# Two fp32r products of a split operand in place of one fp32 product for the row sums of an RWKV-7 recurrence

## The chip, the cores and the metric

One core of a Trainium2 chip. The metric is the device time of one execution in microseconds. Engines are named as the profile names them: PE is TensorE (PEld its weight loads), DVE is VectorE, ACT is ScalarE, POOL is GpSimd, SP is SyncE, which here only issues DMAs.

## What is computed

Two transformer blocks on one sequence of 1024 tokens of width 1024. The first has differential attention beside a diagonal state-space layer and a gated feed-forward; the second has multi-scale retention beside an RWKV-7 recurrence, a gated feed-forward and a gated embedding. All is fp32. The change lies in the RWKV-7 recurrence, which has 8 heads of 64 columns. Two sums over the 64 columns of a head stand in it: the norm of the key, and the bonus.

```python
    kk = k * k_k.reshape(H, N)
    kk = kk * lax.rsqrt(jnp.maximum(jnp.sum(kk * kk, axis=-1, keepdims=True), 1e-24))
    ...
    bonus = jnp.sum(r * k * r_k, axis=-1, keepdims=True) * v
```

## The kernel before

The kernel runs phase after phase. Large matmuls are done as three fp32r products (high by high, high by low, low by high) of operands that were split into a high and a low fp32r part: `split` (L103, L104) writes the high part on ScalarE with an ACTIVATE copy and the low part on VectorE as a subtraction, and `mm3` (L149) issues the three products. Small matmuls of the recurrence are single fp32 products.

`phase_mixers` is the stage of the change. The recurrence is computed in chunks of 64 tokens, on 2 heads at a time: 16 rounds of 4 chunks (4 pairs of heads, 4 quarters of the sequence). Each round goes through four generators: `rw_pre` prepares the round's operands, `rw_solve` inverts a triangular system by substitution and doubling, `rw_chain` carries the state from chunk to chunk, `rw_tail` normalizes and stores. In step i the stage interleaves `rw_pre` of round i, `rw_solve` of round i - 1, `rw_chain` of i - 2 and `rw_tail` of i - 3, and, as filler on TensorE, the retention heads (`ret_all`) and the projections of the next pair of heads (`rw_proj`), whose matmuls are those of L149. `merge` takes turns among the generators by weights (PRN = 40 for `rw_pre`), one `yield` at a time; `ahead` raises the priority of the recurrence's generators. The order on each engine then follows from a scheduler that is run when the kernel is built and that knows dependences, buffers and priorities, so it depends on the whole program.

The rows of a head lie on partitions in `rw_pre`: a tile is 128 partitions (2 heads of 64 columns) by 256 tokens. A sum over a head's columns is therefore a matmul with `C["bones"]`, a 128x128 matrix of ones in two diagonal blocks of 64, and comes out on all 64 partitions. There are two such products in each round. The first (L1475) sums u, the square of the scaled key, written by ScalarE (L1473); its result goes to `d` (L1478), to the reciprocals (L1481), and on to `AR`, `KB`, `AA` and, through a DMA to memory and back, to `A`, on which `rw_solve` of the round begins. The second (L1537) sums u = r * rkw * u (L1535, VectorE), where u before was k times a factor (L1503); its result goes to `bv` (L1540), which only `rw_tail` needs. The tile u has two buffers (UBF = 2). Both results lie in PSUM tiles with the tag `r0`, which has two buffers for `rw_pre`, `rw_solve` and `rw_tail` together. The pool `rw` holds the recurrence's tiles; the pool `rkv`, with the tiles of the projections, lies behind it.

Of the kernel before, what the change touches and what calls it, by code (L numbers as in the profile page):

```python
# [11 lines left out]
F32R = mybir.dt.float32r  # L12
# [54 lines left out]
class Builder:  # L67
# [1351 lines left out]
    def rw_proj(self, pr, hT, pk, pt, ps):  # L1419
# [3 lines left out]
        for i, n in enumerate("rkv"):  # L1423
            ws[n] = self.wunit(self.I["w_rw"][2 + 3 * pr + i])
            for hf in range(2):
# [7 lines left out]
                out[n, hf] = x  # L1433
                yield

    def rw_pre(self, n, p, ps, B, D):


# [2 lines left out]
        nc = self.nc  # L1441
        V, G, AC, TE = nc.vector, nc.gpsimd, nc.scalar, nc.tensor
# [11 lines left out]
        def tmp(tag, bufs=1):  # L1454
            return self.t(p, [128, 256], tag=tag, bufs=bufs)
# [15 lines left out]
        yield  # L1471
        u = tmp("u", UBF)
        AC.activation(u, k, AF.Square, scale=kkw)  # L1473
        pd = self.t(ps, [128, 256], tag="r0", bufs=2)
        TE.matmul(pd, self.C["bones"], u, start=True, stop=True)  # L1475
        yield
        d = tmp("d")
        V.tensor_scalar(d, pd, 1e-24, None, ALU.max)  # L1478
# [21 lines left out]
        u = tmp("u", UBF)  # L1500
# [32 lines left out]
        AC.copy(KBt.rearrange("p c h k -> p c (h k)"), pt)  # L1533
        yield
        V.scalar_tensor_tensor(u, r, rkw, u, ALU.mult, ALU.mult)  # L1535
        pb = self.t(ps, [128, 256], tag="r0", bufs=2)
        TE.matmul(pb, self.C["bones"], u, start=True, stop=True)  # L1537
        yield
        bv = D["bv"] = tmp("bv", BVB)
        V.tensor_tensor(bv, v, pb, ALU.mult)  # L1540
# [325 lines left out]

    def phase_mixers(self, hT):

        with ExitStack() as s:
            p = self.pool("rw", 1, None, s)  # L1870
            pk = self.pool("rkv", 4, None, s)
            ps = self.pool("rwps", 1, PSUM, s)
            B = {}
            B["reset"] = self.load_const("reset", p)
            B["mask"] = self.load_const("rwmask", p).rearrange("p (m t) -> p m t", m=2)
            B["blk"] = self.load_const("rwblk", p).rearrange("p (m b) -> p m b", m=2)
            B["tinit"] = self.load_const("tinit", p).rearrange("p (a b) -> p a b", a=4)
            self.rkv = {}
            D = [{} for _ in range(16)]

            def step(i, *more):
                gens = []
                if 0 <= i - 2 < 16:
                    gens.append((self.ahead(self.rw_chain(i - 2, p, ps, B, D[i - 2]), HC), CHN))
                if 0 <= i - 3 < 16 and i != 16:
                    gens.append((self.ahead(self.rw_tail(i - 3, p, ps, D[i - 3]), HT), TLN))
                if 0 <= i - 1 < 16:
                    gens.append((self.ahead(self.rw_solve(i - 1, p, ps, B, D[i - 1]), HS), SON))
                if i < 16:
                    gens.append((self.ahead(self.rw_pre(i, p, ps, B, D[i]), HP), PRN))  # L1890
                self.merge(gens + [(self.some(g, n), n * FIL) for g, n in more])

            with ExitStack() as s2:
                pw = self.pool("wraw", 1, None, s2, "right") if FINE else None
                self.ws = self.wpool("wD", 2, FINE or 1, s2, "right", pw)
                wr = self.wpool("wR", WRB, FINE or 1, s2, "right", pw)
                pr = self.pool("ret", 1, None, s2, "right")
                self.C2 = {n: self.load_const(n, pr) for n in ("rsc",)}
                ret = self.ahead(self.ret_all(hT, wr, pr, ps), HR) if HR else self.ret_all(hT, wr, pr, ps)
                self.merge([(self.rw_proj(0, hT, pk, pr, ps), 1)])  # L1900
                for i in range(16):
                    if i % 4 == 0 and i < 12:
                        proj = self.rw_proj(i // 4 + 1, hT, pk, pr, ps)
                    step(i, (ret, RS[i]), *([(proj, PJ)] if i < 12 else []))
                self.merge([(ret, 1)])
                self.merge([(self.ahead(self.rw_tail(13, p, ps, D[13]), HT), 1)])
            ct = [self.h_half() for _ in range(2)]
            hT = self.new_hT()
            self.acc = []
            with ExitStack() as s2:  # L1910
                self.acc_half("right")
                self.pn = self.pool("norm", 1, None, self.end, "right")
                self.t(self.pn, [128, 96], tag="pad")
                pe = self.pool("wE", 8, None, s2, "right")
                pws = (pk, "rkv", RKV), (pe, "w"), (pe, "w")
                tags = (("mm", 2), ("mm", 2), ("rt", 2), ("rt", 2))
                early = itertools.chain(
                    self.o_load(0, ct[0], range(8), pk, "rkv", RKV),
                    self.o_half(0, ct[0], pws, (("rkv", RKV),), pk, ps, tags, self.acc, OG),
                    self.o_load(1, ct[1], range(7), pk, "rkv", RKV))  # L1920
                for i in (16, 17, 18):
                    step(i, (early, OE))
                self.merge([(early, 1)])
        return ct[1], hT
# [303 lines left out]
```

## Time and profile before

| | |
|---|---|
| median of 3 runs | 2813.11 us (2798.59 to 2817.27) |
| the profiled execution | 2815.24 us, of which the span is 2813.5 us |
| busy share of the span | PE 96%, PEld 80%, DVE 63%, ACT 40%, POOL 22% |
| mean granted TensorE clock | 0.979 of 2.4 GHz |

The profile is of one execution. Busy times are those of instruction records; a matmul's record is longer than the time for which it holds the array, since matmuls are pipelined, so how far matmuls are apart is read from the starts. Rows of the timeline merge equal instructions that follow one another: the length of such a row reaches from the first one's start to the last one's end.

### The profile page before, as it was taken

How to read it: one execution, taken by the hardware profiler on the slowest of the kernel's cores; microseconds unless marked ns; L12 is line 12 of the kernel's file. 1: busy time of each engine (PE TensorE's matmuls, PEld its weight loads, DVE VectorE, ACT ScalarE, POOL GpSimd, SP SyncE). 2: the span in 40 equal slices, each digit the busy share in tenths (PEclk: the TensorE clock that was granted, in tenths of full speed). 3: DMA queues.
4: the chain of work that ended last, by engine and by line, in shares of the span. 5: the costliest groups of instructions: out<-in, count | busy, mean ns of one | idle time of the engine just before them, and what ended most of it. 6: DMA issues, size and time to landing. Idle time of an engine off the chain costs nothing.

```text
span 2813.5 us, 44349 instructions
## 1 busy us (share of the span) xinstructions
PE 2707.0 (96%) x16624; PEld 2258.4 (80%) x16624; DVE 1763.0 (63%) x3481; ACT 1136.1 (40%) x2210; POOL 627.9 (22%) x1096
## 2 busy tenths in 40 slices
PE   7999998999999999999999999998899999999998
PEld 6988887877888888887787788886787878888887
DVE  6655668377757765464567676766557576665463
ACT  4233566444323344445333333333434233344352
POOL 5024533144111110021132241434031111110010
PEclk9999998999999999999999999999999999999999
DMA  4111020242455566555211111214614555586532
GB/s 144 43 46 48 21 76 23 92 150 90 164 184 175 168 219 236 190 187 188 87 52 43 53 55 47 68 41 135 223 53 135 187 171 170 172 283 204 171 126 85
DMA packets 173807, 352.10 MB, mean 125 GB/s; under 512 B 37784, under 2 KB 83064, under 8 KB 173592
## 3 DMA queue, kind: packets, MB, share of 16 engines
q1 hardware_dynamic: 152248, 277.43, 30.1%
q0 software_dynamic: 21344, 71.84, 7.2%
q8 instruction: 130, 2.13, 0.3%
q14 instruction: 85, 0.70, 0.1%
HBM read 246.90 MB, written 102.30 MB: 124 GB/s over the span
## 4 chain that ended last, share of the span: by engine, by line
PE 68%; issue 11%; DVE 8%; DMA 6%; POOL 3%; ACT 3%; SPq 0%; POOLq 0%; DVEq 0%; ACTq 0%
PE y L149 19%; PE mm L149 15%; PE x L149 7%; PE o L149 6%; PE z L149 5%; PE tr L149 3%; DVE w L104 1%; PE r L1514 1%; PE tr L200 1%; DMA raw<-w_ffn 1%; POOL rp L641 1%; DMA As<-ds 1%; PE o L758 1%; PE u L149 1%; PE r L1604 1%
## 5 line engine op out<-in xcount | busy, mean ns | idle before, releaser
L103 ACT ACTIVATE w<-raw 128x1024 fp32r<-128x1024 f32 (+1 forms) x324 | 286.4, 890 | 418.1 <-PE y L149 147.5
L104 DVE TENSOR_TENSOR w<-raw,w 128x1024 fp32r<-128x1024 f32 (+1 forms) x324 | 331.6, 1028 | 136.3 <-ACT w L103 129.1
L149 PE MATMUL y<-h,w 128*128 128x512 f32 x1152 | 288.6, 392 | 5.4 <-DVE v L353 4.1
L149 PE MATMUL y<-w,h 128*128 128x512 f32 x1152 | 267.3, 391 | 0.0
L149 PE MATMUL mm<-w,h 128*128 128x256 f32 (+1 forms) x1632 | 258.7, 300 | 8.2 <-ACT w L103 7.8
L149 PEld LDWEIGHTS y<-h,w 128*128 128x128 f32 x1152 | 216.5, 189 | 53.1 <-DVE v L353 6.0
L149 PEld LDWEIGHTS y<-w,h 128*128 128x128 f32 x1152 | 215.1, 188 | 44.4 <-ACT mix L1260 0.3
L149 PEld LDWEIGHTS mm<-w,h 128*128 128x128 f32 x1632 | 220.7, 191 | 28.1 <-ACT w L103 8.2
L149 PE MATMUL y<-hx,w 128*128 128x512 f32 x960 | 233.6, 391 | 1.1 <-ACT hx L103 0.9
L149 PEld LDWEIGHTS y<-hx,w 128*128 128x128 f32 x960 | 180.6, 189 | 40.4 <-ACT hx L103 1.8
L149 PE MATMUL mm<-h,w 128*128 128x512 f32 x672 | 188.3, 416 | 6.1 <-ACT w L103 3.0
L104 DVE TENSOR_TENSOR h<-dr,h 128x512 fp32r<-128x512 f32 x154 | 102.3, 687 | 137.5 <-ACT h L103 132.6
L149 PE MATMUL o<-w,h 128*128 128x512 f32 x768 | 182.0, 394 | 2.7 <-DVE mix L1270 1.5
L149 PE MATMUL x<-h,w 128*128 128x512 f32 x672 | 175.3, 392 | 0.0
L149 PEld LDWEIGHTS o<-w,h 128*128 128x128 f32 x768 | 142.5, 188 | 33.1 <-DVE mix L1270 2.2
L103 ACT ACTIVATE h<-dr 128x512 fp32r<-128x512 f32 x154 | 92.6, 624 | 176.3 <-DMA dr<-ff 77.3
L149 PE MATMUL mm<-w,xh 128*128 128x256 f32 x768 | 158.0, 301 | 4.6 <-ACT qk L631 3.4
L149 PEld LDWEIGHTS mm<-h,w 128*128 128x128 f32 x672 | 122.1, 194 | 35.0 <-ACT w L103 4.1
L149 PEld LDWEIGHTS x<-h,w 128*128 128x128 f32 x672 | 124.9, 188 | 26.1 <-ACT w L103 0.9
L149 PE MATMUL z<-h,w 128*128 128x512 f32 x576 | 143.2, 396 | 2.4 <-ACT s L367 1.6
L251 POOL DMA_DIRECT2D ff<-v x66 | 36.4, 551 | 481.6 <-DVE v L361 474.0
L376 DVE TENSOR_TENSOR t<-raw,raw 128x512 f32<-128x512 f32 x40 | 29.8, 744 | 178.0 <-DMA raw<-w_ffn 178.0
(527 smaller groups left out, 5464.8 us busy)
## 6 DMA issues: line engine op xcount, KB each, us to landing
raw<-w_ffn SPq DMA_DIRECT2D x88, 512.0 KB
dr<-ff SPq DMA_DIRECT2D x70, 512.0 KB
ff<-v POOLq DMA_DIRECT2D x88, 256.0 KB, 3.1
td<-w_dn SPq DMA_DIRECT2D x44, 512.0 KB
td<-td POOLq DMA_DIRECT2D x44, 512.0 KB, 3.7
raw<-td SPq DMA_DIRECT2D x40, 512.0 KB
ff<-sd POOLq DMA_DIRECT2D x66, 256.0 KB, 4.8
raw<-w_dn SPq DMA_DIRECT2D x30, 512.0 KB
```

Of the source, the lines that this page charges most:

```text
L103: self.nc.scalar.activation(hi, src, AF.Copy)
L104: self.nc.vector.tensor_tensor(lo, src, hi, ALU.subtract)
L149: return self.nc.tensor.matmul(*a, **kw, skip_group_check=more)
L200: nc.tensor.transpose(p[:, 128 * j : 128 * j + 128], xs[j][:, 128 * k : 128 * k + 128], self.ident)
L251: self.store("v").dma_start(self.part(("ff", {(0, 0): 0, (1, 0): 1, (1, 1): 2}[m, n]), f // 2), v)
L376: V.tensor_tensor(t[:, lo], r[1][:, lo], r[0][:, lo], ALU.subtract)
L641: nc.gpsimd.tensor_tensor(o, a, b, ALU.mult)
L758: nc.tensor.matmul(po, l, r, start=l is am, stop=False)
L1514: TE.matmul(pa[:, c].rearrange("p m t -> p (m t)"), KB[q, c].rearrange("p m s -> p (m s)"), AR[q, c].rearrange("p m t -> p (m t)"), start= ...
L1604: px = per(lambda o, h, c: TE.matmul(o, E[H[h], c], W[H[h], c], start=True, stop=True))
```

## The change

The two fp32 products go through a new helper, `head_sums`. It splits the operand u into an fp32r high part and an fp32r low part (`split`, one instruction on ScalarE and one on VectorE, each 128x256) and issues two fp32r products with the ones, which add up in one PSUM tile. The tiles uh and ul are in the pool `rw`, one buffer each, 1 KB per partition each. The ones are copied to fp32r once at the stage's start (VectorE, 128x128, 512 bytes per partition). Ahead of each of the two PSUM tiles one `yield` is added.

```diff
--- before.py
+++ after.py
@@ -1433,6 +1433,13 @@
                 out[n, hf] = x
                 yield
 
+    def head_sums(self, out, u, p, B):
+
+        uh, ul = (self.t(p, [128, 256], F32R, n) for n in ("uh", "ul"))
+        self.split(uh, ul, u)
+        self.nc.tensor.matmul(out, B["bones"], uh, start=True, stop=False)
+        self.nc.tensor.matmul(out, B["bones"], ul, start=False, stop=True)
+
     def rw_pre(self, n, p, ps, B, D):
 
 
@@ -1471,8 +1478,9 @@
         yield
         u = tmp("u", UBF)
         AC.activation(u, k, AF.Square, scale=kkw)
+        yield
         pd = self.t(ps, [128, 256], tag="r0", bufs=2)
-        TE.matmul(pd, self.C["bones"], u, start=True, stop=True)
+        self.head_sums(pd, u, p, B)
         yield
         d = tmp("d")
         V.tensor_scalar(d, pd, 1e-24, None, ALU.max)
@@ -1533,8 +1541,9 @@
         AC.copy(KBt.rearrange("p c h k -> p c (h k)"), pt)
         yield
         V.scalar_tensor_tensor(u, r, rkw, u, ALU.mult, ALU.mult)
+        yield
         pb = self.t(ps, [128, 256], tag="r0", bufs=2)
-        TE.matmul(pb, self.C["bones"], u, start=True, stop=True)
+        self.head_sums(pb, u, p, B)
         yield
         bv = D["bv"] = tmp("bv", BVB)
         V.tensor_tensor(bv, v, pb, ALU.mult)
@@ -1866,12 +1875,15 @@
 
     def phase_mixers(self, hT):
 
+        nc = self.nc
         with ExitStack() as s:
             p = self.pool("rw", 1, None, s)
             pk = self.pool("rkv", 4, None, s)
             ps = self.pool("rwps", 1, PSUM, s)
             B = {}
             B["reset"] = self.load_const("reset", p)
+            B["bones"] = self.t(p, [128, 128], F32R, "bones")
+            nc.vector.tensor_copy(B["bones"], self.C["bones"])
             B["mask"] = self.load_const("rwmask", p).rearrange("p (m t) -> p m t", m=2)
             B["blk"] = self.load_const("rwblk", p).rearrange("p (m b) -> p m b", m=2)
             B["tinit"] = self.load_const("tinit", p).rearrange("p (a b) -> p a b", a=4)
```

## Rows read from the trace of the kernel before

**Rows 1.** The page: engine shares, and busy tenths in 40 slices of 70 us.

```profile
PE 2707.0 (96%) x16624; PEld 2258.4 (80%) x16624; DVE 1763.0 (63%) x3481; ACT 1136.1 (40%) x2210; POOL 627.9 (22%) x1096
PE   7999998999999999999999999998899999999998
DVE  6655668377757765464567676766557576665463
ACT  4233566444323344445333333333434233344352
```

**Rows 2.** Instructions of L1475 and L1537: durations min/median/max in ns, first and last start.

```profile
L1475 PE MATMUL r<-u,c_bones x32: 376/380/484, 1362.7 to 1883.3; 128*128 128x256 f32 x32
L1537 PE MATMUL r<-u,c_bones x32: 376/379/484, 1379.1 to 1895.5; 128*128 128x256 f32 x32
```

**Rows 3.** Stretches before, in and after the stage: busy time by engine, granted clock.

```profile
core 0: us, PE busy (x) PEld busy (x) DVE busy (x) ACT busy (x) POOL busy (x), PEclk, DMA share, GB/s
1300.00:1360.00 60.00, 53.23 (x207) 38.84 (x206) 20.84 (x32) 28.94 (x56) 2.15 (x7) 0.91 0.43 149
1360.00:1900.00 540.00, 525.92 (x5400) 443.30 (x5399) 379.83 (x1181) 202.48 (x576) 164.84 (x316) 0.99 0.19 53
1900.00:1920.00 20.00, 20.00 (x257) 18.19 (x256) 14.36 (x56) 7.23 (x26) 11.90 (x24) 1.00 0.12 30
1920.00:1980.00 60.00, 44.44 (x435) 33.27 (x435) 32.88 (x78) 23.98 (x64) 17.34 (x35) 0.83 0.57 188
```

**Rows 4.** What TensorE waited for, 1360 to 1900 us: total us, times, longest.

```profile
engine line waited for: us in total, times, longest us
PE r L1604 <- DVE E L1600: 3.1, 2, 1.8
PE rc L1625 <- DVE S L1654: 2.7, 4, 1.7
PE rc L1637 <- ACT X L1633: 1.6, 2, 1.4
PE rt L1767 <- DVE rs_t L1750: 1.4, 1, 1.4
PE rc L1637 <- DVE TT L1607: 1.4, 1, 1.4
PE rt L1787 <- POOL ryy L1784: 1.2, 2, 0.9
PE r L1604 <- DVE Tm L1563: 0.5, 1, 0.5
```

**Rows 5.** Chain of waits, 1360 to 1900 us: shares by engine and line.

```profile
by line: PE mm L149 48.6%; PE r L1514 5.2%; DMA As<-ds 4.6%; PE r L1604 3.6%; DVE Tm L1563 2.1%; PE ry L1658 2.0%; DMA ds<-AA 1.9%; PE r L1693 1.8%; PE rc L1637 1.7%; issue 1.7%; SPq L1523 1.6%; PE r L1475 1.5%; DVE Tt L1564 1.4%; PE rc L16
```

**Rows 6.** Timeline around two old products: start us, us, instruction, count merged.

```profile
1504.17 0.70 PE L1475 MATMUL r<-u,c_bones 128*128 128x256 f32 x2
1504.80 0.27 PE L1604 MATMUL r<-Mt,E 64*64 64x64 f32 x1
...
1519.10 0.60 PE L1537 MATMUL r<-u,c_bones 128*128 128x256 f32 x2
```

**Rows 7.** Timeline: a run of fp32r projection matmuls of the same width.

```profile
1508.27 2.93 PEld L149 LDWEIGHTS mm<-w,h 128*128 128x128 f32 x24
1508.27 3.14 PE L149 MATMUL mm<-w,h 128*128 128x256 f32 x24
```

**Rows 8.** Groups, 1360 to 1900 us: projection matmuls; count | busy us, mean ns.

```profile
L149 PE MATMUL mm<-w,h 128*128 128x256 f32 x1427 | 217.4, 293 | 0.2 <-DVE rg L1805 0.2
L149 PEld LDWEIGHTS mm<-w,h 128*128 128x128 f32 x1428 | 188.3, 190 | 14.2 <-DVE rg L1805 0.6
```

**Rows 9.** Groups, same stretch: the two old products.

```profile
L1475 PE MATMUL r<-u,c_bones 128*128 128x256 f32 x32 | 10.7, 415 | 0.2 <-DVE TT L1607 0.2
L1537 PE MATMUL r<-u,c_bones 128*128 128x256 f32 x32 | 9.7, 386 | 0.3 <-DVE AA L1517 0.3
```

**Rows 10.** Instructions of L103, L104, L1683 and L1503: min/median/max in ns.

```profile
L103 ACT ACTIVATE mh<-gm x1: 311/311/311, 16.7 to 16.7; 128x128 fp32r<-128x128 f32 x1
L103 ACT ACTIVATE h<-dr x154: 610/632/637, 1020.6 to 2689.9; 128x512 fp32r<-128x512 f32 x154
L104 DVE TENSOR_TENSOR ml<-gm,mh x1: 282/282/282, 17.4 to 17.4; 128x128 fp32r<-128x128 f32 x1
L104 DVE TENSOR_TENSOR w<-rkv,w x16: 681/684/687, 1975.9 to 2002.4; 128x512 fp32r<-128x512 f32 x16
L1683 ACT ACTIVATE ysq<-yc x16: 401/417/430, 1467.3 to 1956.3; 128x256 f32<-128x256 f32 x16
L1503 DVE TENSOR_TENSOR u<-rkv,u x16: 414/425/970, 1360.2 to 1868.9; 128x256 f32<-128x256 f32 x16
```

**Rows 11.** Timeline: where u is written, and the later product of the first one.

```profile
1494.22 0.80 DVE L1535 SCALAR_TENSOR_TENSOR u<-rkv,c_rwc,u 128x256 f32<-128x256 f32 x1
1505.63 0.51 ACT L1473 ACTIVATE u<-rkv,c_rwc 128x256 f32<-128x256 f32 x1
...
1536.36 0.59 PE L1475 MATMUL r<-u,c_bones 128*128 128x256 f32 x2
```

## The prediction

> **What bounds the kernel now.** I read the page's engine shares and its forty slices first [rows 1]: TensorE is busy for 96% of the span and 8 or 9 tenths of nearly every slice, VectorE for 63%, ScalarE for 40%. All the changed work lies in one stage: the two product lines that the change edits run from 1362 to 1896 us, 16 products each [rows 2]. So I read the table of stretches next [rows 3]: from 1360 to 1900 us TensorE is busy for 525.9 of 540 us at a granted clock of 0.99, VectorE for 379.8 us (70%), ScalarE for 202.5 us (38%). The rows of what TensorE waited for in that stretch [rows 4] add up to 11.9 us, 9.1 us of it behind VectorE, the longest single wait 1.8 us. The chain of waits there [rows 5] is mostly the projections' matmuls of L149 (48.6%), the filler between the recurrence's short steps; the line that the change touches, L1475, is 1.5% of it, some 8 us. The reader should see a stage in which TensorE's queue sets the pace: work taken off that queue shortens the stage, work put on VectorE or ScalarE is hidden as long as no product comes up in TensorE's queue before its operand is ready. Before and after the stage TensorE is idle for longer: 6.8 of the 60 us before 1360, 15.6 of the 60 us after 1920 [rows 3].
>
> **What is removed and added on TensorE.** An fp32 product of a 128x256 operand shows as two MATMUL records. Of the pair at 1519.10 [rows 6] the two together last 0.60 us and one lasts 0.38 [rows 2], so the second began 0.22 us after the first, and each holds the array for about 0.22. Of the pair at 1504.17 the two last 0.70 us, so the second began 0.32 after the first, and the next matmul of another line began at 1504.80, 0.63 us after the pair's start. So an old product takes 0.44 us where everything is hidden and 0.63 where a step of about 0.1 us shows ahead of its second half and again ahead of what follows. I take the middle, 0.54.
>
> The new product is two fp32r matmuls of the same width. The nearest rows are those of the projections, which have that width and type: 24 of them take 3.14 us [rows 7] at a mean of 0.293 each [rows 8], so they follow one another at (3.14 - 0.29) / 23 = 0.124 us. A pair takes 0.25 us there; that is the bound from below. From above I take 0.44, no better than the best old pair, should each of the two show a step of 0.1 us. I choose 0.29, near the lower end, since width, type and weight loads are those of the filler. The 0.04 on top is the step within the old pairs: the mean records of 0.415 and 0.386 [rows 9] against medians of 0.380 and 0.379 [rows 2] make 0.07 and 0.014 a pair.
>
> There are 32 products. The saving is 32 x (0.54 - 0.29) = 8.0 us; at best 32 x (0.63 - 0.25) = 12.2 us, at worst 32 x (0.44 - 0.44) = 0. The number of TensorE's instructions stays the same, two a product.
>
> **What is added on ScalarE and VectorE.** Each product gets a split: one ACTIVATE (uh) and one subtraction (ul), both 128x256, from SBUF to fp32r. The same two lines have rows at 128x128 and 128x512, 0.311 and 0.632 us on ScalarE, 0.282 and 0.684 us on VectorE, and other instructions of 128x256 on these engines take 0.417 and 0.425, one of them up to 0.970 [rows 10]. I take 0.42 for each; bounds are 0.31 and 0.63 on ScalarE and 0.28 and 0.97 on VectorE. So 32 x 0.42 = 13.4 us go to ScalarE (10 to 20), which rises from 38 to 40% of the stage, and 13.4 us (9 to 31) to VectorE, which rises from 70 to 73% (76 at most). The copy of the ones to fp32r is one more VectorE instruction at the stage's start, 0.28 us by the 128x128 row.
>
> The work that hides the splits is the filler on TensorE, and there is room for them. In the rounds that I followed, a square u is written at 1505.63 and its product starts at 1536.36; a second u is written at 1494.22 and its product starts at 1519.10 [rows 6, 11]. The operands lie ready some 25 to 30 us ahead, because the products wait for their turn on TensorE and for one of two PSUM buffers, not for u. The new uh and ul have one buffer each and both sites share it, so a split can start only after the product of the other site has read it: in this round from 1504.2 to 1519.1 and from 1519.1 to 1536.4, 15 and 17 us for two instructions of 0.42. If that cover were gone, each product would be late by 0.84 us and whatever VectorE has in its queue, and since TensorE takes its matmuls in order, the filler behind it would be late too: 27 us or more. In the old order u's buffer comes free only with the product, now with the subtraction, so the next Square, which goes to the same buffers, isn't later.
>
> What remains is VectorE as a whole: TensorE's 9.1 us of waits behind it grow with its work, by 13.4 / 380 to 31 / 380 of them, 0.3 to 0.7 us, and more where instructions bunch. I put 1 us for that and the copy together. The two added yields only shift the order in which the recurrence's parts are emitted.
>
> **Sum.** The profiled execution took 2815.24 us, 1.7 outside its span. 2815.2 - 8.0 + 1 = 2808 us, 5 below the median of the runs (2813.1) and inside their own spread (2798.6 to 2817.3).
>
> **Rivals.** *Unhidden loads (no change).* Each new matmul needs its weights, and a load lasts 0.19 us [rows 8], longer than the 0.12 us that a matmul holds the array. If a load hid behind the old half product of 0.22 but not behind the new one, a new pair would take the 0.44 of the upper bound, the saving would be nothing and the time 2815 + 1 = 2816. Against it: in the run of 24 the loads are just as long and follow at the same 0.12 us [rows 7]. A rule of the Trainium skill speaks for it: "TensorE: Matmul & The Clock Gate", in Part 3, has weight loads overlap matmuls in flight only where they use other rows of the array, and all rows are used here. By that rule and the page's 107 ns for a load of 128 columns, an estimate for a new pair is 2 x (107 + 107) = 430 ns. The run of 24 does not bear the rule out.
>
> *Hidden gain (no change).* The stage's end is set by the recurrence and the stores behind it, which leave TensorE idle for 15.6 us after 1920 [rows 3]: filler that ends 8 us sooner only waits longer there. For it: that idle. Against it: TensorE is busy for all of the 20 us before [rows 3]. Time: 2815 + 1 = 2816.
>
> *Late subtraction (slower).* Place: TensorE's queue at the 32 products. They all wait for VectorE now, the busiest of the other engines, where before half of them waited for ScalarE. Price: half of the longest wait behind VectorE that the trace shows, 0.9 us [rows 4], at each product: 32 x 0.9 = 28.8, so 2815.2 - 8.0 + 28.8 = 2836. It decides from 0.25 us a product, where the gain is used up, and would be over 1% slower from (28 + 8) / 32 = 1.1 us. For it: the pair's one buffer, and VectorE at 73%. Against it: 15 us of room, and that waits behind VectorE are few and short where it is at 70% [rows 4].
>
> *Another order.* The order on all engines is worked out anew when the kernel is built, with two more yields in each round and 2.5 KB more in the pool in front. The idle at the stage's end, 15.6 us [rows 3], can shrink or grow by about itself: 2808 - 15.6 = 2792 or 2808 + 15.6 = 2824. Over 1% faster would need the best saving (12.2) and nearly all of this idle together.
>
> **Chances.** Forecast 0.50, from 2803 to 2816 by the bounds of the saving; unhidden loads 0.05; hidden gain 0.10; another order, lower 0.12, higher 0.10; late subtraction 0.13. The likeliest gives 2808. The range for 8 in 10 goes from just under the lower order, 2789, to the late subtraction's price, 2836. About 1% (28 us) is what a measurement of this kernel can tell from no change. Under 2785 lies only the tail of the lower order, 0.05; over 2841 the upper part of the late subtraction and of the higher order, 0.10; within 1% the rest, 0.85.
>
> **What the changed profile would show.** Right: 32 pairs of fp32r matmuls on the new helper's lines, the second some 0.12 us after the first; 32 rows each of L103 and L104 at 128x256, about 0.42 us long; TensorE waiting for ul for no more than an us or two in total, and for everything in the stage for some 12 us; VectorE about 13 us busier; the recurrence's last tail some 8 us sooner. Wrong: waits of the new products for ul of many us (late subtraction); pairs 0.2 us apart (unhidden loads); the stage's filler done sooner but its last stores not (hidden gain); TensorE's idle after 1920 or before 1360 changed by over 8 us (another order).

## The result and the profile after

The changed kernel took 2827.9 us (median of 7 runs, 2821.7 to 2832.5) against 2810.0 us for the kernel before (7 runs, 2798.6 to 2817.3): a ratio of 1.0063, interval 1.0047 to 1.0079. It is 13 to 22 us slower. That lies inside the predicted range and within 1%, but on the other side of the forecast, which was 7 us below the profiled execution of before.

The profiled execution of after took 2821.71 us (span 2819.9), only 6.5 us more than that of before. The two pages differ little; the first two lines answer to [rows 1]:

```profile
PE 2704.5 (96%) x16624; PEld 2256.7 (80%) x16624; DVE 1772.6 (63%) x3514; ACT 1149.9 (41%) x2242; POOL 635.0 (23%) x1096
PE   7998998999999999999999999998899999999998
```

TensorE's count is unchanged, VectorE and ScalarE have the 33 and 32 instructions that were added, and TensorE is busy for 2.5 us less. The loss must be read from the stage. Up to it the two kernels do the same work, and this execution of after came to it 6.6 us earlier (1330.6 us in place of 1337.2), so times since the span's start mislead. I take the stage from the last copy of the low-rank projections (L1416) to the first addition of the output projection (L1864, in after L1873). The stretch table of before, columns as in [rows 3]:

```profile
1337.20:1963.40 626.20, 604.43 (x6149) 506.49 (x6148) 426.05 (x1314) 234.94 (x675) 194.91 (x376) 0.98 0.21 62
```

and of after:

```profile
1330.60:1972.80 642.20, 610.35 (x6152) 511.87 (x6151) 435.90 (x1346) 247.43 (x707) 201.95 (x376) 0.98 0.21 61
```

The stage is 16.0 us longer at the same granted clock of 0.98 (the 2.4 GHz level for nearly all of it). VectorE is busier by 9.9 us and ScalarE by 12.5, as added. But TensorE, which was to have 8 us less, is busy for 5.9 us more and idle for 31.9 us in place of 21.8. The lateness swings as it grows: counted from the stage's start, the state update S (L1654 before, L1663 after) begins for the 16th time 3 us later than before, for the 32nd and the 48th 11, for the 54th 8.5, for the 56th and last 17.5. So a good part of it arises in the middle, and a good part in the last two updates.

What TensorE waited for in after from 1360 to 1900 us, to be held against [rows 4]:

```profile
PE r L1613 <- DVE E L1609: 6.1, 3, 3.5
PE mm L149 <- DVE rg L1814: 3.0, 2, 2.4
PE rc L1634 <- DVE S L1663: 2.3, 3, 1.2
PE ry L1667 <- ACT VU L1648: 1.9, 2, 1.3
PE mm L149 <- DVE w L104: 1.5, 1, 1.5
PE r L1601 <- DVE AA L1525: 1.3, 2, 0.7
PE mm L149 <- ACT re L1728: 1.0, 2, 0.6
```

All eleven rows add up to 19.2 us; the view of before has fifteen, which add up to 13.7 ([rows 4] shows the first seven, 11.9). None is a wait of the new products (L1440, L1441). The waits that grew belong to instructions that the change doesn't touch, the triangular inverse above all: L1613 waits for E, 6.1 us in place of the 3.1 of L1604 in [rows 4]. The new instructions are as long as forecast:

```profile
L103 ACT ACTIVATE uh<-u x32: 400/418/447, 1351.9 to 1882.7; 128x256 fp32r<-128x256 f32 x32
L104 DVE TENSOR_TENSOR ul<-u,uh x32: 407/421/967, 1352.9 to 1883.8; 128x256 fp32r<-128x256 f32 x32
```

What waited for them and for the product, by the same view (line, us, times):

```profile
  ACT u L1480: 16.4, 8
  ACT uh L103: 15.5, 13
```

The copy to uh waited 15.5 us for the product that still read the one uh, and the Square that writes u (L1480) waited 16.4 us for the subtraction. Before, the Square waited less, and for the product:

```profile
L1473 ACT ACTIVATE u<-rkv,c_rwc x16: 492/508/510, 1359.0 to 1854.1; 128x256 f32<-128x256 f32 x16
...
  PE r L1475: 4.2, 7
```

### The profile page after: what moved, and what is told of

Read it like the earlier page. It is cut to its first block, busy times and chain, and to the rows that moved or that the text cites. A ratio compares the mean times of both kernels' runs of the same rounds, so it can differ in the third digit from the quotient of the medians.

```text
span 2819.9 us, 44349 instructions
## 1 busy us (share of the span) xinstructions
PE 2704.5 (96%) x16624; PEld 2256.7 (80%) x16624; DVE 1772.6 (63%) x3514; ACT 1149.9 (41%) x2242; POOL 635.0 (23%) x1096
## 4 chain that ended last, share of the span: by engine, by line
PE 64%; issue 11%; DVE 11%; DMA 7%; POOL 3%; ACT 3%; SPq 1%; POOLq 0%; DVEq 0%; ACTq 0%
PE y L149 19%; PE mm L149 12%; PE x L149 7%; PE o L149 6%; PE z L149 6%; PE tr L149 3%; DMA raw<-w_ffn 2%; DVE w L104 2%; DMA As<-ds 1%; PE tr L200 1%; POOL rp L641 1%; PE u L149 1%; PE o L758 1%; PE r L1522 1%; ACT w L103 1%
## 5 line engine op out<-in xcount | busy, mean ns | idle before, releaser
L103 ACT ACTIVATE w<-raw 128x1024 fp32r<-128x1024 f32 (+1 forms) x324 | 286.8, 891 | 413.1 <-PE y L149 133.8
L104 DVE TENSOR_TENSOR w<-raw,w 128x1024 fp32r<-128x1024 f32 (+1 forms) x324 | 332.2, 1030 | 124.7 <-ACT w L103 117.2
L104 DVE TENSOR_TENSOR h<-dr,h 128x512 fp32r<-128x512 f32 x154 | 102.6, 688 | 139.3 <-ACT h L103 133.1
L103 ACT ACTIVATE h<-dr 128x512 fp32r<-128x512 f32 x154 | 92.9, 626 | 178.2 <-DMA dr<-ff 74.2
```

Source lines behind the costliest of these rows:

```text
L103: self.nc.scalar.activation(hi, src, AF.Copy)
L104: self.nc.vector.tensor_tensor(lo, src, hi, ALU.subtract)
```

## The experiments

Four theories stood at the start. **A**: the one buffer each of uh and ul holds ScalarE up, and what it does next comes late. **B**: the change has the order on all engines worked out anew, and the new order is worse than the old, whatever the work. **C**: the added work itself costs that much. **D**: the 2.5 KB more in the pool move other tensors, and the place costs. All ratios are to runs of the kernel before on the same chip; 0.1% is 2.8 us. Stage, busy and idle are TensorE's, in us, in one profiled execution each; before and e8_room, which have one order, differ by 1.3 us in the stage and by 2.5 in idle. An order is "free" where the scheduler works it out, and "held" where it is fixed as explained below.

| run | work | order | ratio (interval) | stage | busy | idle |
|---|---|---|---|---|---|---|
| before | old | old | 1 | 626.2 | 604.4 | 21.8 |
| after | new | new | 1.0063 (1.0047 to 1.0079) | 642.2 | 610.4 | 31.9 |
| e1_yield | old | free, two yields | 1.0046 (1.0034 to 1.0058) | 631.7 | 610.4 | 21.3 |
| e2_noyield | new | free, no yields | 1.0056 (1.0041 to 1.0071) | 633.2 | 607.3 | 25.9 |
| e3_split | splits alone | free, two yields | 1.0056 (1.0044 to 1.0068) | 647.7 | 620.6 | 27.1 |
| e4_product | products alone | free, two yields | 1.0032 (1.0022 to 1.0041) | 634.1 | 606.6 | 27.5 |
| e8_room | old, 2.5 KB more | old | 1.0004 (0.9994 to 1.0014) | 624.9 | 605.6 | 19.3 |
| e5_old_order | new | old, held | 1.0009 (0.9999 to 1.0020) | 625.7 | 601.0 | 24.7 |
| e6_old_order_product | products alone | old, held | 0.9999 (0.9990 to 1.0008) | 628.6 | 605.8 | 22.8 |
| e7_new_order | old | after's, held on three engines | 1.0113 (1.0096 to 1.0131) | 654.4 | 618.5 | 35.9 |
| e9_triple_product | old product three times | old, held | 1.0077 (1.0059 to 1.0094) | 645.7 | 627.7 | 18.0 |
| e10_triple_split | new, each split three times | old, held | 1.0044 (1.0027 to 1.0061) | 632.3 | 604.8 | 27.5 |
| e11_prn42 | old | free, one weight moved | 1.0018 (1.0006 to 1.0030) | 627.0 | 602.5 | 24.5 |
| e12_change_prn | new | free, one weight moved | 1.0052 (1.0034 to 1.0071) | 642.7 | 611.3 | 31.4 |
| e13_hold_pe | new | old on TensorE alone | 1.0063 (1.0045 to 1.0081) | 643.1 | 605.4 | 37.7 |
| e14_hold_dve | new | old on VectorE alone | 1.0143 (1.0123 to 1.0163) | 664.2 | 616.0 | 48.2 |
| e15_hold_rest | new | old on all but TensorE | 1.0035 (1.0021 to 1.0049) | 635.3 | 604.5 | 30.8 |
| e16_hold_aps | new | old on ScalarE, GpSimd, SyncE | 1.0082 (1.0065 to 1.0098) | 646.9 | 610.5 | 36.4 |

### One part of the change at a time, the order free

**The yields alone**, with before's work:

```diff
         AC.activation(u, k, AF.Square, scale=kkw)
+        yield
...
         V.scalar_tensor_tensor(u, r, rkw, u, ALU.mult, ALU.mult)
+        yield
```

> The kernel before with the two yields alone: no split, one fp32 product at each site. Theory A (the split holds ScalarE up: uh and ul have one buffer and both sites share it, so ScalarE waits with the next split for the product of the other site, and the next Square waits for the subtraction; the recurrence's copies stand behind them): no split, no such wait, the time of before, 2810 within 5. Theory B (another order: any edit of the stage makes the order on all engines come out anew, and the one of before was a good one): 2815 to 2830, without any work added. Theory C (the added work of 13 us each on ScalarE and VectorE itself): 2810 within 5.

Measured +0.46%, 13 us, with not one instruction added or changed. TensorE's busy time is after's (610.4) though its matmuls are before's, and its idle time is before's (21.3). In this execution, the fastest of its five, the stage is only 5.5 us longer, at a granted clock of 0.99 in place of 0.98, and all of that is busy time.

**The change without its yields** (the same two lines taken out of after):

> The changed kernel without its two yields. Theory A and theory C: the splits are all there, so the time of the changed kernel, 2828 within 5. Theory B: another order again, so a time that differs from 2828 by more than 5, to either side; if the yields were the cause of the order, near 2805 to 2812.

Measured +0.56%. The yields are enough for the loss, but not needed: the new instructions alone bring another order too.

**The splits without the new products** (uh and ul are written, and read by nobody):

```diff
-        self.nc.tensor.matmul(out, B["bones"], uh, start=True, stop=False)
-        self.nc.tensor.matmul(out, B["bones"], ul, start=False, stop=True)
+        self.nc.tensor.matmul(out, self.C["bones"], u, start=True, stop=True)
```

> The changed kernel with its splits and yields, but the products stay single fp32 products of u, so that uh and ul are written and read by nobody (the result is that of before). uh and ul come free with the subtraction, not with a product. Theory A: ScalarE does not wait for TensorE for uh any more, so most of the loss is gone: 2812 to 2818. Theory C: the added work is all there and the 8 us that TensorE saves are not: 2828 + 8 = 2836. Theory B: anything from 2805 to 2835.

**The new products without the splits**: u is written as fp32r by its producers, both products read it with ones of 0.5, and the low part of u is left out:

```diff
...
+        self.nc.tensor.matmul(out, B["bones"], u, start=True, stop=False)
+        self.nc.tensor.matmul(out, B["bones"], u, start=False, stop=True)
...
-        V.scalar_tensor_tensor(u, r, rkw, u, ALU.mult, ALU.mult)
+        ur = self.t(p, [128, 256], F32R, "ul")
+        V.scalar_tensor_tensor(ur, r, rkw, u, ALU.mult, ALU.mult)
...
+            nc.vector.tensor_scalar(B["bones"], self.C["bones"], 0.5, None, ALU.mult)
```

> The products alone: u is written in fp32r by its producers, each site has its own tile, and the two fp32r products both read it with ones halved, so the low part is left out and no split runs. TensorE's saving is there, nothing is added on ScalarE or VectorE. Theory A and theory C: 2810 - 8 = 2802. Theory B: not below 2808, since the order comes out anew here too.

Measured +0.56% and +0.32%. Even products that add nothing to any other engine lose when the order is free. Beside the yields alone, the splits add 0.10% and the products take off 0.14%: little beside the 0.46% that another order costs without any work. C can't explain that. The differences aren't prices of the parts, though, since each of these kernels has its own order.

**The room alone**, an unused tile of 2.5 KB in the same pool (the order of every engine but GpSimd's one extra instruction stays before's):

```diff
+            self.nc.gpsimd.memset(self.t(p, [128, 640], tag="room")[:, 0:1], 0.0)
```

> The kernel before with an unused tile of 2.5 KB in the pool rw (one element of it is set to zero on GpSimd), so that the tiles behind it lie where they lie in the changed kernel. The order on TensorE, VectorE, ScalarE and SyncE is that of before. All theories: 2804 within 4. If it is slower by 10 or more, the place in memory is what costs (a fourth theory, D).

Measured 1.0004, its interval from -0.06 to +0.14%: D falls.

### The order held

Here every instruction of an engine that before has too is tied to the one that stood before it there, by an edge that fixes the order and waits for nothing on the chip. The added instructions (splits, second products, the copy of the ones) have no such edge. The core of it:

```diff
+        for step in array.array("h", zlib.decompress(base64.b85decode(text))):
+            at += step
+            i = made[at]
...
+            if last is not None:
+                b.tc.add_manual_dep(i, last.name, mybir.DependencyInfo(
+                    mybir.DependencyClass.NoSync, mybir.DependencyReason.DATA), reason="order")
+            last = i
```

**The whole change in before's order**, without yields, and **the products alone in it** (low part left out again):

> The whole change (split, two fp32r products, fp32r ones, 2.5 KB more; without the two yields) with the order of the kernel before held on all five engines by order-only edges; only the added instructions stand where the scheduler finds room. On this chip before takes 2804. Theory B (the order alone makes the loss): TensorE's saving of 8 us shows, 2796 to 2800. Theory A (the split's buffer and the Square's wait hold ScalarE up) and theory C (the added work itself): the loss stays, 2814 to 2822.

> The products alone in the order of before, held in the same way: the producers write u in fp32r, both products read it with ones halved, the low part is left out, no split. All theories: TensorE's saving without added work, 2804 - 8 = 2796. If it is 2804 or more, the saving itself is no gain (hidden gain). The difference from e5 is the price of the splits in a fixed order: theory B 0 to 4, theory C 18 and more.

Measured +0.09% and -0.01%. The same splits, the same single buffers and the same products that lose 18 us in the new order lose some 2.5 us in the old one. That is the case's main result: B. It also bounds A: with the same one buffer of uh, the copy waits 5.6 us for the product in this order, not 15.5, so most of those waits come with the order. Two buffers each, the direct removal, weren't tried.

**Before's work in after's order** (two yields; TensorE, ScalarE and SyncE held to the order of after, but for the Square and the first write of the second u; VectorE and GpSimd free):

> The work of the kernel before (one fp32 product at each site, no split), with the two yields, and with TensorE, ScalarE and SyncE held to the order of the changed kernel (its added instructions taken out; the Square and the first write of the second u are left free, since u's buffers come free later here). Theory B: the loss comes with the order, 2815 to 2830. Theory A and theory C: 2804 within 5.

Measured +1.13%, more than after itself. Without one new instruction this order costs 32 us. It isn't after's in full, since VectorE and GpSimd have an order of their own here, so it shows that an order close to after's is slow without the work, not what after's own order costs. In the stretch table the stage has 654.4 us:

```profile
1337.50:1991.90 654.40, 618.51 (x6141) 513.98 (x6140) 427.67 (x1313) 234.79 (x675) 193.32 (x376) 0.97 0.20 59
```

**One weight**, `rw_pre`'s turn among the generators, PRN 40 to 42, with before's work, and 42.5 with the change:

```diff
-CHN=28;SON=47;PRN=40;...
+CHN=28;SON=47;PRN=42;...
```

> The kernel before with the weight of rw_pre among the generators 42 in place of 40: no work is added or taken away, no tile moves, only the order comes out anew. Theory B (any other order costs): 2812 to 2825. If orders come out as often better as worse, 2796 to 2816; theory A and theory C: 2806 within 4.

> The changed kernel with the weight of rw_pre 42.5 in place of 40, so that its 34 steps take as long a share of a round as the 32 steps of before did. If the two yields' slower pace of rw_pre made the order bad: back to 2806 to 2812. Theory B in its plain form (any order but the tuned one): another time between 2806 and 2835, with no relation to the pace. Theory A and theory C: 2824 within 5.

Measured +0.18% and +0.52%: another order of the old work is slower again, and this one other order of the new work isn't better than after's (intervals overlap).

**Which engine's order?** The change without yields, with before's order on some engines only:

> The whole change without its yields, as in e2 and e5, with the order of before held on TensorE alone; VectorE, ScalarE, GpSimd and SyncE come out anew. With no engine held (e2) it took 0.56% more than before, with all five held (e5) 0.09%. If the loss comes from TensorE's own order (filler and steps put in another turn): near e5, 0.0 to 0.2%. If it comes from the other engines' order: near e2, 0.4 to 0.6%.

> The same with the order of before held on VectorE alone. If VectorE's order, on which TensorE's products wait, is the cause: near e5, 0.0 to 0.2%. If TensorE's: near e2, 0.4 to 0.6%.

> The same with the order held on VectorE, ScalarE, GpSimd and SyncE, and TensorE left free (some 1,200 of its 14,280 matmuls then stand elsewhere than in e5). If TensorE's own order is the cause: 0.3 to 0.6%. If the other engines' order is: 0.0 to 0.2%.

> The same with the order held on ScalarE, GpSimd and SyncE, and TensorE and VectorE left free. If the two free engines' orders are the cause: 0.4 to 0.6%. If ScalarE's or the DMAs' order is: 0.0 to 0.2%.

No single engine carries it. TensorE held alone is as slow as after, VectorE alone costs 1.43%, and of the sets tried only all five together come to 0.09%. In e13_hold_pe TensorE is busy for only 605.4 us, but idle for 37.7: it has the old order, and its operands come in another one. That the orders have to fit each other is the reading of these four runs; which pair of engines matters was not tried.

**The granted clock** is a rival, since the clock records show TensorE at 1.2 GHz in some stretches of the stage. Averaged over all runs it is 0.979 and 0.980 of 2.4 GHz in e1_yield and e3_split and 0.979 in before on the same chip, so their loss isn't the clock's; after has 0.978. e7_new_order, e14_hold_dve and e16_hold_aps have 0.975, 0.974 and 0.975: by an estimate from these means, up to 0.4 to 0.5% of their 0.8 to 1.4% is time lost at the lower clock.

### The prices of the terms, the order held

**The old product three times** (64 products more, same output), and **each split three times** (64 instructions more on each of ScalarE and VectorE):

```diff
+        for _ in range(2):
+            self.added.add(TE.matmul(pd, self.C["bones"], u, start=True, stop=True).ins.name)
...
+        for _ in range(3):
+            for i in (nc.scalar.activation(uh, u, AF.Copy), nc.vector.tensor_tensor(ul, u, uh, ALU.subtract)):
```

> The kernel before with each fp32 product issued three times into the same tile (the same result), in the order of before held by order-only edges: 64 more products on TensorE, nothing else. An old product holds the array for 0.47 us in the traces, so 64 of them are 30 us. If the stage is bound by TensorE's queue as the prediction took it: 2806 + 30 = 2836. If TensorE's time there is mostly hidden (hidden gain): 2806 to 2816.

> The whole change in the order of before, held, with each split issued three times (64 more ACTIVATEs of 0.42 us and 64 more subtractions of 0.42 us, 27 us on each engine; the same result). e5, with each split once, was within 3 us of before. If the added work is hidden, as theory B has it: within 6 us of e5, 2808 to 2816. Theory C: each round of 13 us costs as much as the first, and it would show here doubled, 2830 and more.

64 more old products of 0.435 us (see below) are 27.8 us on TensorE; the time rose by 0.77%, 21.6 us (16.6 to 26.4). Some 0.8 of what is put on TensorE's queue reaches the end, so the reading of the bound was right. Two more rounds of splits cost 0.0044 - 0.0009 = 0.35%, 9.8 us (4 to 16), about 5 us a round, though all that the products waited for them directly in e10_triple_split is 0.4 us. But the repeats share one uh, so each copy has to wait for the subtraction that still reads it, which the single split doesn't:

```profile
L1463 ACT ACTIVATE uh<-u x96: 400/417/449, 1352.3 to 1886.8; 128x256 fp32r<-128x256 f32 x96
...
  DVE ul L1463: 34.7, 29
```

With these 34.7 us of ScalarE's waiting, 5 us is rather an upper figure for a round. The single round is e5_old_order against e6_old_order_product: 0.10%, 2.8 us (-1 to 7).

### What a product costs depends on its neighbours

The old product between two small matmuls takes 0.63 us, from 1504.17 to 1504.80 in [rows 6]. Between projection matmuls of the same kernel:

```profile
1465.68 0.64 PE L149 MATMUL mm<-w,h 128*128 128x256 f32 x4
1466.16 0.59 PE L1475 MATMUL r<-u,c_bones 128*128 128x256 f32 x2
1466.41 0.83 PE L149 MATMUL mm<-w,h 128*128 128x256 f32 x4
```

The next run begins 0.25 us after the product, and its four take 0.83 us in place of 0.64, so the product costs 0.25 + 0.19 = 0.44 us. The new pair in after, in the timeline of matmuls and loads, stands between small ones:

```profile
1527.87 0.19 PEld L1606 LDWEIGHTS r<-Mt,AA 64*64 64x64 f32 x2
1527.88 0.33 PE L1606 MATMUL r<-Mt,AA 64*64 64x64 f32 x2
...
1528.13 0.19 PEld L1440 LDWEIGHTS r<-uh,bones 128*128 128x128 f32 x1
1528.13 0.39 PE L1440 MATMUL r<-uh,bones 128*128 128x256 f32 x1
...
1528.24 0.19 PEld L1441 LDWEIGHTS r<-ul,bones 128*128 128x128 f32 x1
1528.35 0.28 PE L1441 MATMUL r<-ul,bones 128*128 128x256 f32 x1
...
1528.56 0.33 PE L1606 MATMUL r<-Mt,AA 64*64 64x64 f32 x4
```

0.22 us to the second, 0.21 more to what follows, 0.43 in all; and the load of the first begins with its matmul, not ahead of it. In e5_old_order (L1464 and L1465 are the pair, L171 the projections) one stands between projections:

```profile
1462.02 0.76 PE L171 MATMUL mm<-w,h 128*128 128x256 f32 x5
...
1462.50 0.19 PEld L1464 LDWEIGHTS r<-uh,bones 128*128 128x128 f32 x1
1462.62 0.28 PE L1464 MATMUL r<-uh,bones 128*128 128x256 f32 x1
1462.62 0.19 PEld L1465 LDWEIGHTS r<-ul,bones 128*128 128x128 f32 x1
1462.74 0.28 PE L1465 MATMUL r<-ul,bones 128*128 128x256 f32 x1
...
1462.86 0.64 PE L171 MATMUL mm<-w,h 128*128 128x256 f32 x4
```

0.12 us apart, 0.24 in all, and each load begins 0.12 us ahead of its matmul. Worked out in this way for all 32 products from the records of TensorE (what other matmuls between the two halves took is left out):

| | between 128x128 tiles | one neighbour smaller | between smaller tiles | 32 products, us |
|---|---|---|---|---|
| old product, us each (before) | 0.435 | 0.53 | 0.63 | |
| new pair, us each (e5_old_order) | 0.24 | 0.33 | 0.43 | |
| products so placed: before | 12 | 9 | 11 | 17.3 |
| e1_yield (old product) | 2 | 7 | 23 | 19.4 |
| e7_new_order (old product) | 3 | 2 | 27 | 19.7 |
| after | 4 | 1 | 27 | 14.4 |
| e2_noyield (new pair) | 11 | 10 | 11 | 13.0 |
| e5_old_order (new pair) | 13 | 9 | 10 | 12.1 |

Each change of tile next to the product costs 0.1 us, for the old product and the new alike. The pair saves 0.2 us wherever it stands, unless its halves are parted: in five pairs each of after and e5_old_order other matmuls stand between them, and so their sums are above those by the prices. And after's order, like that of the yields alone, puts 27 (23) of the 32 among the small matmuls, where before had 11: 2 us of its gain go there. In the whole stage TensorE goes from one form of matmul (tile and columns) to another 759 times before, 764 times in e5_old_order, and 813 times after (802 with the yields alone). At about 0.1 us each the 54 more would be some 5 us, an estimate from the table. TensorE is busier by 5.9 us although the pairs save it 2.9, so that is over half of the 8.8 us to be explained. It isn't the whole account: e3_split has 823 such changes and 16 us more.

## Why the prediction was right or wrong

**What bounds the stage: right.** e9_triple_product shows that TensorE's queue sets the pace. The reading that followed from it, that work on the other engines is hidden as long as no product is late, was too simple: in e10_triple_split the products waited 0.4 us for their splits, and the 64 more splits, with the waits that they make for each other, still cost 9.8 us.

**The old product: right.** 0.44 to 0.63 us, 0.54 in the mean; the 32 take 17.3 us, 0.54 each.

**The new pair: mis-sized.** I took 0.29 us, the price between projection matmuls (0.25; measured 0.24) with 0.04 for the step. But I had priced the old product with its steps among small matmuls, and the new one almost without. In the old order the pair takes 0.38 us in the mean, and the saving is 17.3 - 12.1 = 5.2 us, not 8.0; after's is 17.3 - 14.4 = 2.9. The rule of the Trainium skill that stood beside this ("TensorE: Matmul & The Clock Gate", Part 3, loads overlap only where they use other rows) gave an estimate of 0.43. That number was met, between small matmuls, but by another sum: 0.24 and two steps of 0.1. Between projections loads of all rows do run ahead; so here it is the change of tile that holds a load back, and the rule as worded is not what the rows show.

**The splits: durations right, price not settled.** 0.418 and 0.421 us against 0.42. "I put 1 us" lies within the -1 to 7 us measured for one round, below its middle of 2.8. e5_old_order, the whole change in the old order, has +2.5 us (-0.3 to 5.6). e6_old_order_product, which has the saving without the splits, shows at most 2.8 us of the 5.2, so **hidden gain** can't be ruled out for a part, although e9_triple_product has 0.8 of TensorE's time count. The granted clock took some of it: 0.978 in the mean of its runs against 0.979, at most some 2 us by an estimate. Where the rest of the saving went is not settled.

**"The next Square isn't later": wrong in after.** Its waits grew from 4.2 us to 16.4. That this sets the time is not shown: with the order held, the same buffers cost next to nothing.

**"The two added yields only shift the order": the step that failed.** I named another order as a rival, but priced it by the idle at the stage's end and gave its slower side 0.10. It is the whole sign of the result. The yields alone cost 13 us, the same change in the old order 2.5, so the new order costs 0.63 - 0.09 = 0.54%, some 15 us. It isn't the idle that I priced: in the windows of [rows 3] TensorE is idle for 15.0 us from 1920 to 1980 in after, for 15.6 before, while from 1360 to 1900 it is idle for 19.6 in place of 14.1:

```profile
1360.00:1900.00 540.00, 520.43 (x5360) 439.90 (x5358) 383.87 (x1197) 209.94 (x599) 168.74 (x311) 0.99 0.19 53
...
1920.00:1980.00 60.00, 45.05 (x446) 34.32 (x444) 26.90 (x73) 19.78 (x60) 19.69 (x39) 0.86 0.48 152
```

The last window runs past the stage's end, though. From 1920 us to that end the two kernels have, before and after,

```profile
1920.00:1963.40 43.40, 38.71 (x418) 29.39 (x418) 25.08 (x67) 17.84 (x55) 16.14 (x32) 0.88 0.49 161
```

```profile
1920.00:1972.80 52.80, 43.82 (x440) 33.57 (x439) 24.81 (x68) 19.41 (x59) 18.03 (x36) 0.87 0.41 135
```

so TensorE is idle there for 9.0 us in place of 4.7. Of the 10 us more idle, 5.5 lie in the middle and 4.3 at the end; the rest of the 16 us is busy time, to which the rival gave no price at all. That its slower time, 2824, is near the measured one is luck.

And the chances weren't even: of the twelve kernels timed in another order (after, e1 to e4, e7, e11 to e16), none was faster than before, where I had given 0.12 to the faster side.

**Late subtraction: the wrong mechanism for the right sign.** TensorE never waited for ul. **Unhidden loads**: its price of 0.44 a pair was met at most places of after, for the reason above, and the time went up by more than that.

**Left open.** Which meetings of operands in after's order make TensorE wait 10 us longer, and why e3_split and e7_new_order keep TensorE busy for 16 and 14 us more. A part of these is the clock. At the 1.2 GHz level, where the projection matmuls of [rows 7] follow one another at 0.21 us in place of 0.12 (a run of e14_hold_dve at a granted clock of 0.50),

```profile
1593.59 2.76 PE L171 MATMUL mm<-w,h 128*128 128x256 f32 x12
```

TensorE is busy for 29 us of the stage in e3_split and 31 in e7_new_order, for 19 before and 16.5 in after. At half the rate the 10 and 12 us more are 5 and 6 us of lost time, an estimate; the other 11 and 8 us stay open, and after's 5.9 us are not the clock's.

## What to carry to other kernels

Where a kernel's order is worked out anew at each build, a change of a few us must first be priced as a change of order: put a change that does nothing (a yield, a weight) beside it, and run the change itself with the old order held. Price an instruction at the place where it will stand: the steps that the old one pays to its neighbours are paid by the new one too. And if the order can be held, hold it on all engines, since holding one of them alone was no better than none (TensorE) or worse (VectorE).

## What the runs showed of the hardware

A matmul on the whole array that follows one on a smaller tile has its weight load begin with it, not 0.12 us ahead: in the records of before, the 98 of 128x256 behind a 64x64 tile and the 23 behind a 128x64 tile start 2 ns after their load began (median), those behind one of their own form 0.117 us after. In this stage the spacing of a 128x256 fp32r pair goes from 0.12 to 0.22 us, and the next small matmul comes 0.21 us after it in place of 0.12. An old fp32 product pays the same 0.1 us at each side (0.435, 0.53, 0.63 us). Which matmuls stand next to each other is thus a cost of its own on TensorE, and it isn't read from durations (0.38 to 0.48 us for an old half [rows 2]) but from where the next matmuls start.
